# A hybrid attention / mLSTM layer on one core: the hand-over from the last head's scan to the output projection, rearranged

## The chip, the cores and the metric

The kernel runs on one core of a Trainium2 chip. The metric is the device time of one execution in microseconds (us); lower is better. Before the change the median of three runs is 1529.1 us (1527.36 to 1534.01).

A core has five engines that run side by side, each through its own list of instructions in a fixed order: PE (TensorE, matrix products into the eight PSUM banks), DVE (VectorE), ACT (ScalarE), POOL (GpSimd) and SP (SyncE, which here only issues DMA transfers). ACT and POOL issue some transfers too. An instruction whose input, or whose memory, is not yet free stops its engine and all that stands behind it in the list.

## The reference, cut to what matters

One layer works on 128 context tokens and 1024 latent tokens of width 1024, nine blocks of 128 rows; block 0 is the context. A conditioning vector gives six modulation vectors (shift, scale and gate, for each of two sub-layers), one set for context and one for latent tokens:

```python
m = jax.nn.silu(cond) @ w_ada_l + b_ada_l          # split into sh1, sc1, g1, sh2, sc2, g2
h = rmsnorm(x, norm1_w) * (1 + sc1) + sh1
...                                                # attention heads and mLSTM heads side by side, from h @ w_in
mix = jnp.concatenate([attn_o, hm], axis=-1) @ w_out
x = x + g1 * mix
h2 = rmsnorm(x, norm2_w) * (1 + sc2) + sh2
x = x + g2 * swiglu(h2, w_gu, w_down)
```

The mLSTM heads run a scan in both directions over the blocks; their result, normalised and gated, is `hm`. The first half of the rows of `w_out` belongs to attention, the second to the mLSTM heads.

## The kernel before, in words

The nine blocks are taken in three groups ("c") of three. Matrix operands are split into a high and a low part, and a product is the sum of three. The stages in order of time: modulation, first norm and the input projections; four mLSTM heads, head by head (projection, then scan), with attention for group 0 beside them; then, around 440 to 570 us of the profile, the hand-over with which the change deals; then for each group the gated feed-forward (`gate_up`, `down`), with attention and the output projection of the next group beside it.

The hand-over has these parts, which are written as Python generators and interleaved:

- The scan of the last head (`head_mlstm`). Its rows `hm` go out to memory in DRAM by POOL's queue in the end (L965).
- `attn_out_first`: the attention half of the output projection for group 0. It takes two scratch tiles in the place of two tiles of normalised input that are no longer needed: `gta` (six pieces of 128 x 512 floats: pieces 0 and 1 the gates g1 of the first 512 columns for context and latent rows, 2 and 3 those of the second, 4 the product, 5 the padded conditioning vector) and `mxa` (the split attention output of three blocks). DVE multiplies the bank by the gate into piece 4 (L1360), POOL adds that to the rows `x1a` (L1361). Later, pieces 0 and 1 serve as the landing place `spare` for weights.
- `ada_rest((5,), ...)`: the last modulation vector, g2, in two halves of 512. Each half ends with a row: a DMA on SP's queue loads the bias into the row (L477), DVE adds the product to it (L480) and halves it (L482), and ACT's queue stores it to DRAM (L483). Both halves use the same row `hmx[0:2, 512:1024]`, so the second bias load waits until the first row has been stored.
- `prefill`: the mLSTM half of the output projection for all nine blocks. For a block b, `mix(b)` turns the rows `hmr` (PE transposes, L120) and splits them into a tile `mx` (ACT L1265, DVE L141); `half(b, n)` makes the products of 512 columns (`out_block`, L1219, L1221, L1223), multiplies by the gate out of the bank into a tile `t` (`add_gated`, DVE L1180) and adds it to the rows (POOL L1181). The gate of block 0 is `gx_all`, that of the others `gl`. `end(b)` takes the squares of the rows for the second norm (`stats`, ACT L1398). `norm2` scales a block's rows (ACT L1414), turns them (PE L120), applies scale and shift (ACT L1422, DVE L1424) and splits the result (ACT L1429, and POOL for group 0, L141); before, block 0 to 2 follow `end(2)` to `end(4)`.
- `attention` for group 1 begins beside `prefill`. It loads a block's queries into a tile `qr` of which there is one (ACT's queue, L1078), turns and splits them (`qT`, L1089), and for each head makes the scores (PE L1111), their maximum (DVE L1113), the exponentials into a tile `pr` of which there are two (ACT L1114), and a split copy (ACT L1117, DVE L1118), which DMA transposes for the value products.

Two things set the order. First, a planner lays the instructions of each engine in a fixed order before the run, from its own estimate of their durations; `hot(n)` lets the instructions in its block count as n places earlier, and `issue_after` puts some behind others. Second, tiles lie in pools, and a pool's memory is used again when it has been closed. The pools of the hand-over are laid from the lower end in the order of their opening, so the tiles of `prefill` come to lie on those of `attn_out_first`; a new tile waits until the tiles under it have been read for the last time. From their sizes, in KB of each partition, counted from the start of the old input tiles:

| place | tile of `attn_out_first` | tile of `prefill`, before | `attn_out_first`, after | `prefill`, after |
|---|---|---|---|---|
| 0 to 8 | `mxa`, blocks 0 and 1 | `wq`, split weights | `gta`, pieces 0 to 3 | `wq` |
| 8 to 12 | `mxa`, block 2 | `mx`, first (`gx_all`) | `gta`, pieces 4 and 5 | `hmr`, both |
| 12 to 20 | `gta`, pieces 0 to 3 | `mx`, second and third | `mxa`, blocks 0 and 1 | `mx`, first and second |
| 20 to 24 | `gta`, pieces 4 and 5 | `hmr`, both | `mxa`, block 2 | `mx`, third |

The tiles `t` of `add_gated` come from the pool `ft` at the other end of the memory, three of them under the tag `t2`; that place was held by tiles of earlier stages.

## Time and profile before

| | us |
|---|---|
| median of three runs | 1529.1 |
| lowest and highest | 1527.36, 1534.01 |
| the profiled execution: its time | 1531.07 |
| the profiled execution: its span, first to last instruction | 1529.3 |
| PE busy in the span | 1473.0 |
| DVE, ACT, POOL busy | 1015.8, 770.4, 268.8 |
| granted clock, mean | 0.989 |

The profile is of one execution. In its rows a start is in us from the start of the span, then comes a duration, the engine, the line of the kernel, the operation, and the tiles as output<-inputs; buffer numbers are left out, so all tiles of one name share a row. What stands in brackets is the time that the engine sat idle before, and the instruction that ended the wait. "SPq" or "ACTq" is the issue of a transfer on that engine's queue; the transfer itself lands later. An `f32` product takes several passes, so one of them can count as more than one instruction. The rows by window give for each engine its busy time and, in parentheses, its instructions; then the clock that PE was granted (1.00 is full), the share of the DMA engines' time, and GB/s.

### The profile page before, as it was taken

How to read it: one execution, taken by the hardware profiler on the slowest of the kernel's cores; microseconds unless marked ns; L12 is line 12 of the kernel's file. 1: busy time of each engine (PE TensorE's matmuls, PEld its weight loads, DVE VectorE, ACT ScalarE, POOL GpSimd, SP SyncE). 2: the span in 40 equal slices, each digit the busy share in tenths (PEclk: the TensorE clock that was granted, in tenths of full speed). 3: DMA queues.
4: the chain of work that ended last, by engine and by line, in shares of the span. 5: the costliest groups of instructions: out<-in, count | busy, mean ns of one | idle time of the engine just before them, and what ended most of it. 6: DMA issues, size and time to landing. Idle time of an engine off the chain costs nothing.

```text
span 1529.3 us, 23410 instructions
## 1 busy us (share of the span) xinstructions
PE 1473.0 (96%) x8539; PEld 1244.7 (81%) x8539; DVE 1015.8 (66%) x2025; ACT 770.4 (50%) x1429; POOL 268.8 (18%) x354
## 2 busy tenths in 40 slices
PE   6899999999998899999999999999999999999997
PEld 3545567677766789999898999989998989999996
DVE  4887654838568866878637587787866585554554
ACT  4764475947654645556433444656553443323333
POOL 0113423333344441010010100100010101101110
PEclk9899999999999999999999999999999999999998
DMA  9664323523456577869635357886864445544541
GB/s 359 205 198 147 101 71 42 120 53 62 110 177 207 135 180 187 200 156 195 171 115 166 124 184 212 198 184 145 201 145 138 138 139 179 158 135 126 153 144 56
DMA packets 387113, 233.77 MB, mean 153 GB/s; under 512 B 170102, under 2 KB 347462, under 8 KB 386998
## 3 DMA queue, kind: packets, MB, share of 16 engines
q1 hardware_dynamic: 385006, 228.69, 55.0%
q10 hardware_dynamic: 1864, 3.20, 0.9%
q8 instruction: 67, 1.10, 0.3%
q14 instruction: 48, 0.39, 0.1%
q0 software_dynamic: 128, 0.39, 0.1%
HBM read 182.21 MB, written 11.69 MB: 127 GB/s over the span
## 4 chain that ended last, share of the span: by engine, by line
PE 78%; DVE 5%; DMA 3%; ACT 3%; issue 1%; POOL 1%; SPq 0%; ACTq 0%; DVEq 0%; POOLq 0%
PE mm L1437 11%; PE mm L1436 11%; PE mm L1435 11%; PE mm L1191 5%; PE mm L1192 5%; PE mm L1193 5%; PE S L1111 4%; PE wi L514 3%; PE wi L513 3%; PE wi L512 3%; PE mm L1219 2%; PE po L1136 2%; PE po L1135 2%; PE mm L1221 2%; PE mm L1223 2%
## 5 line engine op out<-in xcount | busy, mean ns | idle before, releaser
L163 ACT CAST whi<-raw 128x1024 fp32r<-128x1024 f32 x214 | 219.2, 1026 | 367.8 <-PE mm L1436 146.9
L141 DVE TENSOR_TENSOR wlo<-raw,whi 128x1024 fp32r<-128x1024 f32 x214 | 257.7, 1204 | 170.5 <-ACT whi L163 167.0
L1436 PE MATMUL mm<-aTl,whi 128*128 128x384 f32 x1056 | 354.4, 336 | 0.0
L1437 PE MATMUL mm<-aTh,wlo 128*128 128x384 f32 x1056 | 354.2, 336 | 0.0
L1435 PE MATMUL mm<-aTh,whi 128*128 128x384 f32 x1056 | 353.2, 335 | 0.0
L141 POOL TENSOR_TENSOR hl<-tn,hl 128x384 fp32r<-128x384 f32 x66 | 84.9, 1286 | 846.6 <-ACT hl L1458 796.4
L1435 PEld LDWEIGHTS mm<-aTh,whi 128*128 128x128 f32 x1056 | 198.3, 188 | 0.7
L1436 PEld LDWEIGHTS mm<-aTl,whi 128*128 128x128 f32 x1056 | 198.3, 188 | 0.6
L1437 PEld LDWEIGHTS mm<-aTh,wlo 128*128 128x128 f32 x1056 | 198.3, 188 | 0.1
L1191 PE MATMUL mm<-whi,hl 128*128 128x512 f32 x372 | 144.4, 392 | 1.1 <-DVE t L1180 1.1
L1192 PE MATMUL mm<-wlo,hl 128*128 128x512 f32 x372 | 145.1, 391 | 0.0
L1193 PE MATMUL mm<-whi,hl 128*128 128x512 f32 x372 | 142.7, 391 | 0.0
L1118 DVE SCALAR_TENSOR_TENSOR pl<-pr,st,ph 128x1152 f16<-128x1152 f32 (+1 forms) x72 | 96.9, 1346 | 37.3 <-ACT ph L1117 35.9
L1113 DVE TENSOR_REDUCE st<-S 128x1 f32<-128x1152 f32 (+1 forms) x72 | 88.9, 1234 | 17.5 <-PE S L1111 17.2
L1114 ACT ACTIVATE pr<-S,st 128x1152 f32<-128x1152 f32 (+1 forms) x72 | 81.3, 1129 | 33.0 <-DVE st L1113 28.2
L1117 ACT ACTIVATE ph<-pr,st 128x1152 f16<-128x1152 f32 (+1 forms) x72 | 83.8, 1164 | 26.3 <-issue 10.9
L1180 DVE TENSOR_TENSOR t<-mm,gl 128x512 f32<-128x512 f32 x102 | 69.1, 686 | 38.1 <-PE mm L1193 16.0
L512 PE MATMUL wi<-headw,hT 128*128 128x384 f16 x288 | 93.9, 326 | 0.2 <-ACT th L799 0.2
L513 PE MATMUL wi<-headw,hT 128*128 128x384 f16 x288 | 93.9, 326 | 0.0
L514 PE MATMUL wi<-headw,hT 128*128 128x384 f16 x288 | 93.9, 326 | 0.0
L1111 PE MATMUL S<-kst,qT 128*128 128x384 f32 (+1 forms) x400 | 84.5, 344 | 0.8 <-ACT pr L1114 0.8
L1191 PEld LDWEIGHTS mm<-whi,hl 128*128 128x128 f32 x372 | 69.9, 188 | 15.2 <-DVE t L1180 1.5
(400 smaller groups left out, 2591.3 us busy)
## 6 DMA issues: line engine op xcount, KB each, us to landing
raw<-in_w_gu_dram SPq DMA_DIRECT2D x132, 512.0 KB
raw<-in_w_down_dram SPq DMA_DIRECT2D x60, 512.0 KB
a<-in_w_ada_dram SPq DMA_DIRECT2D x24, 512.0 KB
gl<-g_d SPq DMA_DIRECT2D x36, 256.0 KB
aw<-in_w_ada_dram SPq DMA_DIRECT2D x16, 512.0 KB
iraw<-in_w_in_dram SPq DMA_DIRECT2D x32, 256.0 KB
x<-in_x_sample_dram SPq DMA_DIRECT2D x11, 512.0 KB
raw<-in_w_out_dram SPq DMA_DIRECT2D x10, 512.0 KB
```

The lines of the kernel that those rows point to most:

```text
L141: (dve if eng == "dve" else pool).tensor_tensor(out=out, in0=full, in1=hi, op=ALU.subtract)
L163: nc.scalar.copy(hi[:, :n], raw[:, :n])
L512: mm(ps[:, :n], ah, wh[:, k % 2, c0 : c0 + n], start=(k == 0), stop=False)
L513: mm(ps[:, :n], ah, wl[:, k % 2, c0 : c0 + n], start=False, stop=False)
L514: mm(ps[:, :n], al, wh[:, k % 2, c0 : c0 + n], start=False, stop=(k == KD - 1))
L1111: mm(S[:, n, 0:w], qT[:, h, :], kst[kv][:, t, c0 + n * w : c0 + (n + 1) * w], start=(t == 0), stop=(t == 1))
L1191: mm(ps, ah, wh[:, k % 2, :], start=(k == 0), stop=False)
L1192: mm(ps, ah, wl[:, k % 2, :], start=False, stop=False)
L1193: mm(ps, al, wh[:, k % 2, :], start=False, stop=(k == nk - 1))
L1435: mm(ps, wh[:, k, :], th[:, k, :], start=(k == 0), stop=False)
L1436: mm(ps, wh[:, k, :], tl[:, k, :], start=False, stop=False)
L1437: mm(ps, wl[:, k, :], th[:, k, :], start=False, stop=(k == KD - 1))
```

## The change

1. In `attn_out_first` the second bias row no longer takes the row of the first, but the first two partitions of a tile under the tag `qr`, attention's only query tile.
2. The pool of the old input tiles becomes two, opened in the order 1, 0, so `gta` and `mxa` change places; the rows `hmr` get a pool of their own, opened ahead of that of `mx`. The table above shows both.
3. The products `t` of blocks 0 and 1 in `prefill` go into two tiles under attention's tag `pr`, one for each half of the columns, block 0 in the first 512 columns of it and block 1 in the next.
4. `norm2` of blocks 0, 1 and 2 no longer follows `end(2)`, `end(3)` and `end(4)`, but `half(3, 0)`, `half(4, 0)` and `half(5, 0)`, that is half a block later in program order.

```diff
-    hTp = es1.enter_context(tc.tile_pool(name="hTp", bufs=1, reuse_waits="tile"))
+    hTp = [es1.enter_context(tc.tile_pool(name=f"hTp{c}", bufs=1, reuse_waits="tile")) for c in (1, 0)][::-1]
...
-    hT = [(hTp if c < 2 else rowp).tile([P, 2, KD, CT], F16, name=f"hT{c}", tag=f"hT{c}" if c < 2 else "b4") for c in range(NCH)]
+    hT = [(hTp[c] if c < 2 else rowp).tile([P, 2, KD, CT], F16, name=f"hT{c}", tag=f"hT{c}" if c < 2 else "b4") for c in range(NCH)]
...
-    def add_gated(x1, ps, g, n, eng=dve):
+    def add_gated(x1, ps, g, n, eng=dve, t=None):
         cs = slice(n * 512, (n + 1) * 512)
-        t = t2()
+        t = t2() if t is None else t
...
-            hm = xe.tile([P, 512], F32, name=nm("hmr"), tag="hmr", bufs=2)
+            hm = xh.tile([P, 512], F32, name=nm("hmr"), tag="hmr", bufs=2)
...
             if c < 2:
-                add_gated(x1s[c][i], ps, g, n, pool)
+                if b < 2:
+                    if b == 0:
+                        mixed["t", n] = ap2.tile([P, 3, CT], F32, name=nm("t2"), tag="pr", bufs=2).rearrange("p a n -> p (a n)")
+                    t = mixed["t", n][:, b * 512 : (b + 1) * 512]
+                else:
+                    t = None
+                add_gated(x1s[c][i], ps, g, n, pool, t)
...
-            if 2 <= b < CB + 2:
-                yield from norm2(0, cur, b - 2)
...
-        yield from end(0)
+        end(0)
...
-        yield from end(1)
+        end(1)
         for b in range(2, NB):
             load_x1(b + 2)
             half(b, 0)
             yield
+            if 3 <= b < CB + 3:
+                yield from norm2(0, cur, b - 3)
             if b + 1 < NB:
                 mix(b + 1)
                 yield
             half(b, 1)
             yield
-            yield from end(b)
+            end(b)
...
-        gt = hTp.tile([P, 6, 512], F32, name="gta", tag="hT1")
-        mx = hTp.tile([P, CB, NQ, P], F32R, name="mxa", tag="hT0")
+        gt = hTp[1].tile([P, 6, 512], F32, name="gta", tag="hT1")
+        mx = hTp[0].tile([P, CB, NQ, P], F32R, name="mxa", tag="hT0")
...
+        rows_at = [lambda: hmx[0:2, 512:1024],
+                   lambda: ap.tile([P, NQ, HD], F32, name="bias", tag="qr", bufs=1).rearrange("p h d -> p (h d)")[0:2]]
...
-                       lambda: hmx[:, 0:512], lambda: hmx[0:2, 512:1024], 1, store=nc.scalar.dma_start)
+                       lambda: hmx[:, 0:512], lambda: rows_at.pop(0)(), 1, store=nc.scalar.dma_start)
...
     homes["wq"] = ctx.enter_context(tc.tile_pool(name="wq", bufs=1, reuse_waits="tile"))
+    xh = ctx.enter_context(tc.tile_pool(name="xh", bufs=1, reuse_waits="tile"))
     xe = ctx.enter_context(tc.tile_pool(name="xe", bufs=1, reuse_waits="tile"))
```

## The prediction

> **What bounds the kernel now.** I read the page's first part, then the busy time in long stretches.
>
> ```profile
> PE 1473.0 (96%) x8539; PEld 1244.7 (81%) x8539; DVE 1015.8 (66%) x2025; ACT 770.4 (50%) x1429; POOL 268.8 (18%) x354
> ```
>
> ```profile
> 500.00:530.00 30.00, 26.36 (x116) 21.21 (x117) 25.53 (x67) 18.30 (x29) 14.81 (x10) 0.89 0.63 153
> 518.00:526.00 8.00, 7.42 (x25) 6.00 (x24) 5.15 (x20) 5.98 (x10) 3.48 (x3) 0.57 0.34 81
> 600.00:900.00 300.00, 300.00 (x1641) 275.93 (x1640) 204.31 (x296) 139.37 (x183) 24.43 (x19) 1.00 0.63 160
> ```
>
> The columns are length, then PE, PEld, DVE, ACT and POOL busy, the granted clock, DMA. From 600 to 900 PE never idles and has its full clock, so an edit there could win only by fewer matmuls, and this change removes none. A stall that goes ahead of such a stretch is kept to the end. The edits lie at 455 to 545, where the last head's scan hands over to the output projection (prefill). There PE idles 3.64 of 30 us and the clock falls to 0.57. So I read PE's timeline there; brackets give idle time and releaser.
>
> ```profile
> 482.09 1.07 PE L1223 MATMUL mm<-ir,mxa 128*128 128x512 f32 x4
> ...
> 485.37 0.66 PE L120 MATMUL mm<-ident,hmra 128*128 128x128 f32 x4
> 486.10 0.68 PE L936 MATMUL wi<-va,sd 128*128 128x129 f32 x4
> 488.60 1.19 PE L1219 MATMUL mm<-whi,mx 128*128 128x512 f32 x4 [1.81 <-ACT mx L1265]
> ...
> 490.91 1.18 PE L1223 MATMUL mm<-whi,mx 128*128 128x512 f32 x4
> 491.92 0.60 PE L120 MATMUL mm<-ident,qr 128*128 128x128 f32 x4
> ...
> 496.95 1.07 PE L1223 MATMUL mm<-whi,mx 128*128 128x512 f32 x4
> ...
> 501.12 1.20 PE L1219 MATMUL mm<-whi,mx 128*128 128x512 f32 x4 [1.61 <-DVE mx L141]
> ...
> 517.17 1.55 PE L120 MATMUL mm<-ident,y 128*128 128x128 f32 x8 [1.82 <-ACT y L1414]
> ...
> 520.15 2.04 PE L1219 MATMUL mm<-whi,mx 128*128 128x512 f32 x4 [0.57 <-DVE fl L1424]
> ...
> 567.70 0.33 PE L1435 MATMUL mm<-aTh,whi 128*128 128x384 f32 x1
> ```
>
> Four waits, 5.81 us in all: for mixing operands (1.81 and 1.61), for block 0's normalised rows (1.82), and for a bank that norm2 still holds (0.57). The half clock costs 8.00 x (1 - 0.57) = 3.4 us more. These 9.2 us are all that closing the stalls named here can give.
>
> **The change part by part.** No arithmetic instruction is added or removed; waits and places change.
>
> *First four products (t in pr).* An output block leaves its PSUM bank by DVE L1180 into a t2 tile, then POOL adds it.
>
> ```profile
> 501.93 0.67 DVE L1180 TENSOR_TENSOR t<-mm,gx_all 128x512 f32<-128x512 f32 x1
> ```
>
> ```profile
> 485.37 1.27 POOL L1361 TENSOR_TENSOR x1a<-x1a,gta 128x512 f32<-128x512 f32 x1 [0.80 <-DVE gta L1360]
> ...
> 499.03 0.58 POOL L965 DMA_DIRECT2D hm_d<-hm  x1 [0.42 <-POOL hm L960]
> 502.69 7.15 POOL L1181 TENSOR_TENSOR x1a<-x1a,t 128x512 f32<-128x512 f32 x4 [3.08 <-DVE st L1116]
> ...
> 540.29 2.55 POOL L141 TENSOR_TENSOR aTl<-fl,aTh 128x512 fp32r<-128x512 f32 x2 [1.55 <-ACT aTh L1429]
> ```
>
> ```profile
> hm_d<-hm POOLq DMA_DIRECT2D x2, 192.0 KB, 2.3
> ```
>
> The first output block left PE at 492.1 (490.91 + 1.18), yet its product ran at 501.93. The t2 memory lies at the right-hand end, where the last head's rows were: their store went out at 499.03 and lands 2.3 us later, 501.3. That reads as the wait. In a pr tile, idle since attention's block 2, the first product can run at about 492.5, the third when its block ends at 498.0 (496.95 + 1.07); the second needs gl, asked for at 492.6 (row below). So the banks come free some 4 to 9 us sooner and the wait of 1.61 at 501 goes: value 1.6, bounds 0 and 1.6. POOL's four adds, 502.69 to 509.84, start with them, and so do the statistics of block 0 (ACT, with the casts of which the next part speaks):
>
> ```profile
> 486.21 1.04 ACT L163 CAST whi<-raw 128x1024 fp32r<-128x1024 f32 x1 [1.95 <-DMA raw<-in_w_out_dram]
> ...
> 487.96 0.58 ACT L1265 CAST mx<-mm 128x512 fp32r<-128x512 f32 x1
> ...
> 500.51 1.22 ACT L1114 ACTIVATE pr<-S,st 128x1152 f32<-128x1152 f32 x1 [0.37 <-DVE st L1113]
> ...
> 508.63 1.06 ACT L1398 ACTIVATE jk<-x1a 128x1024 bf16<-128x1024 f32 x1 [4.61 <-POOL x1a L1181]
> ...
> 516.41 1.32 ACT L1414 ACTIVATE y<-x1a,ry 128x512 f32<-128x512 f32 x2
> ```
>
> The square waited 4.61 us for POOL; its result reached y at 516.41, 7.8 us after it began. If the square starts at about 501.5, y comes near 509.3, and PE at 515 doesn't wait for it: 1.82 + 0.57 = 2.4, bounds 0 and 2.4.
>
> What this adds: the first two heads' exponentials (ACT, L1114) wait for the pr tiles until the POOL adds of those t are done; behind them in ACT's queue stand casts and squares, for which DVE and PE wait. The first head's tile needs two adds of about 1.8 (7.15 for four), begun near 493 and 498, so done near 500; its exponential starts at 500.51 now. Covered: 0, bounds 0 and a loss of the second gap's 1.6.
>
> *norm2 half a block later.* Its instructions stay 800 places ahead in priority, so the planner puts them where their inputs are ready, as before; I take 0. Bounds: a gain of 1.8 (already in the term above) and no loss, because gate_up, the reader, begins at 567.70, 25 us after the last norm2 subtraction ends at 542.84 (540.29 + 2.55).
>
> *Places exchanged.* Mixing tile 0 lay on the gates' tile gta, last read by POOL until 486.64 (485.37 + 1.27). After, it lies on mxa, last read by PE until 483.16 (482.09 + 1.07). So block 0's ACT cast can run when its transposes end, 486.03, instead of 487.96, if the planner puts it ahead of the weight cast at 486.21, which sat on ACT waiting for its DMA. Ahead: PE starts by 486.7 and the whole 1.81 goes. Behind: nothing. I take half, 0.9. The weight cast would run 0.58 later, for output blocks that come after 492: 0. The weight slot wq, after the change on the gates, is free at 486.64; the second of the two weight casts of this pair, which uses it, can't start before the first's end at 487.25: 0. The hmr tiles stay on the same parts of gta, so their issue at 486.67 stays.
>
> *Second bias row in the query tile.*
>
> ```profile
> 466.10 1.02 SPq L1369 DMA_DIRECT2D hmra<-hm_d  x2
> 468.77 0.27 SPq L477 DMA_DIRECT2D hmx<-in_b_ada_dram  x1
> 469.09 0.39 SPq L162 DMA_DIRECT2D gta<-in_w_out_dram  x1
> 486.67 0.34 SPq L1236 DMA_DIRECT2D hmr<-hm_d  x1
> 492.60 0.84 SPq L1211 DMA_DIRECT2D gl<-g_d  x2
> ```
>
> ```profile
> 468.33 0.69 DVE L1360 TENSOR_TENSOR gta<-mm,gta 128x512 f32<-128x512 f32 x1 [0.44 <-PE mm L1223]
> ```
>
> SP stands from 467.12 to 468.77 (1.65) for the first row's store. Behind it is the load into gta, which must wait anyway for the last reader of those gates, until 469.02: it was issued at 469.09. So 0; the upper bound is 1.6. On the other side, the query tile was loaded far ahead:
>
> ```profile
> 345.74 0.33 ACTq L1078 DMA_DIRECT2D qr<-q_d  x1
> ```
>
> ```profile
> 489.15 0.25 ACTq L483 DMA_DIRECT2D g_d<-hmx  x1
> ```
>
> ```profile
> 476.52 3.71 DMA gta<-in_w_out_dram
> ```
>
> If the bias row takes the slot first, the load has to follow the row's store: 489.15 + 2.3 (the nearest store) + 3.7 (the nearest load, twice as large) = 495.2, and attention's transposes, at 491.92 today, come 3.3 us later. PE then has the output blocks up to 498 to do, if they are ahead in its queue; ACT, which issues the load, would stand up to 2.3 with casts behind it. I take 0; bounds 0 and a loss of 3.3 plus another half clock.
>
> *The sum.* 1.6 + 2.4 + 3.4 = 7.4 is what PE could save in 500 to 530. But DVE is busy 25.53 of those 30 us, a share of 0.85. Three products of 0.67 move ahead of 500, leaving 23.5, which doesn't fit into 22.6. I take a share halfway between 0.85 and 1, 0.925: 23.5 / 0.925 = 25.4 us. So I count 30 - 25.4 = 4.6 and the 0.9: 5.5. Against the profiled execution's 1531.07 (span 1529.3 and 1.8 around it) that is 1525.6. That execution lies 2.0 above the median of the runs, 1529.1, so I carry the difference over: **1523.6**.
>
> *A rule of the clock.* The granted clock fell to 0.51 in 518 to 520, after this:
>
> ```profile
> 486.00:488.00 2.00, 0.71 (x5) 0.52 (x4) 1.93 (x5) 1.79 (x5) 0.64 (x1) 1.00 0.97 387
> 488.00:490.00 2.00, 1.40 (x6) 1.18 (x7) 2.00 (x5) 1.75 (x5) 0.00 (x0) 1.00 0.85 261
> 514.00:516.00 2.00, 1.35 (x8) 0.99 (x6) 1.73 (x15) 1.79 (x2) 0.00 (x0) 1.00 0.00 0
> 516.00:518.00 2.00, 0.83 (x6) 0.63 (x7) 2.00 (x5) 1.87 (x5) 0.33 (x1) 1.00 0.99 120
> 518.00:520.00 2.00, 1.57 (x8) 1.17 (x6) 2.00 (x7) 1.17 (x3) 0.94 (x1) 0.51 0.87 180
> ```
>
> PE was busy 2.11 of 4 us at 486 to 490 and kept its clock, 2.18 of 4 at 514 to 518 and lost it. So a gap of that size costs the clock once in two here, and closing it is a chance, not a certainty. The Trainium skill, TensorE: Matmul & The Clock Gate, "HAM oscillation", puts the rule at no idle gaps over about 3.4 us. By it the 1.82 us gap would not be the cause, and closing it would leave the half clock: at most 1.6 + 2.4 + 0.9 = 4.9 saved, 1524.2, and the second rival would weigh more. The trace disagrees with the plain rule, as no gap here is that long; the page's free-running window would fit the two unlike outcomes.
>
> **The rivals.** (1) *All closes*: attention's share of DVE's work slips behind 530, where PE has other work, and PE saves 0.9 + 0.9 + 7.4 = 9.2: 1519.9. For it: in 600 to 900 DVE is busy 204 of 300, so there is room to catch up. Against: block 0's chain to y runs through DVE too. (2) *The clock still drops*, because another wait (for a mixing operand or attention's first scores) takes its place: only about 1.5 stays, 1527.6. For it: ACT and DVE are nearly full there. (3) *Slower, through the query tile*: PE meets attention's transposes in its queue before their rows have landed. Price 3.3 and a half clock of 3.4 with no gap closed: 1535.8. It decides if the planner leaves them ahead of output blocks 2 and 3, at 491.9, and the rows land later than 492; each us past that costs one. (4) *The planner's order shifts further on*: its estimated timeline moves, and a later hand-over (there are two more) gets a wait and a clock drop like those of 515, 5.8 each; both give +11.6 - 5.5 = +6.1, 1535.2; with the third rival's 3.3, 1538.5. Against: PE is full for hundreds of us around them. (5) *The change does not do what it says*, because the waits have other causes: 1529.
>
> **How the numbers follow.** The forecast and its neighbours (1521.5 to 1526) 0.42; all closes 0.14; clock still drops or no effect 0.20; query tile 0.13; shifted order 0.11. 0.5% is 7.6 us, about what a measurement of this kernel can tell from no change: below 1521.5 only the first rival, 0.14; above 1536.7 the tails of the third and fourth, 0.16 with what I can't see in the planner's order; between, 0.70. The range 1519 to 1537 leaves out about 0.05 below and 0.15 above. The forecast's own range is 1521 to 1526.
>
> **What would show it.** Right: the first L1180 near 492 to 494 and the fourth before 503; POOL's first adds before 500; y of block 0 before 511; no half clock between 510 and 530; the bias row issued near 467; the first L1219 on mx at 486.7 (place exchange worked) or 488.6 (it didn't); gate_up's first matmul about 5 us before 567.7 and the same span behind it. Wrong: PE waiting for qr at 492 or ACT standing behind its load; first products still at 502 (then another tile held them); a half clock elsewhere in 480 to 567; or new PE idle time after 600.

## The result, and the profile after

The kernel after takes 1534.8 us (median of 12 runs, 1532.4 to 1538.13); the kernel before, run beside it on the same chip, takes 1530.84 us (12 runs, 1527.36 to 1534.23). The ratio is **1.003, 95% interval [1.0019, 1.0041]**. That is 4.0 us slower, where 5.5 us less were forecast. The time lies in the range that was given, 1519 to 1537, but the change has the other sign. The profiled execution of after took 1534.57 us, its span is 3.5 us longer than that of before:

```profile
span 1532.8 us, 23405 instructions
...
PE 1473.3 (96%) x8539; PEld 1244.0 (81%) x8539; DVE 1023.2 (67%) x2025; ACT 769.9 (50%) x1429; POOL 270.8 (18%) x354
```

PE has the same work (1473.3 against 1473.0 us), so all but 0.3 of the 3.5 us is idle time. DVE, with the same 2025 instructions, is busy 7.4 us longer. That becomes a clue below.

The start of the hand-over itself moves by up to 4.6 us from one profile to the next (481.96 to 486.57 in the 20 kernels' profiles). The clock ahead of it is a large part of that: counted as length x (1 - granted clock), its drops up to the mark cost 8.5 us in after and 13.7 in after_later, whose mark is the latest, with the same idle time of 36 us. So stages have to be compared from a mark of their own. I use three marks on PE: the end of the last product on `mxa` (483.16 before), the first `gate_up` product (567.70) and the first `down` product (606.23); a fourth, the first transposes of the next norm2, at 874.38. The columns are those of the rows by window in the prediction. First before, then after:

```profile
483.16:567.70 84.54, 78.53 (x400) 63.24 (x400) 66.59 (x149) 45.08 (x74) 38.57 (x29) 0.96 0.66 169
567.70:606.23 38.53, 38.09 (x228) 37.40 (x227) 22.01 (x29) 18.98 (x25) 5.54 (x5) 1.00 0.69 194
```

```profile
482.41:569.62 87.21, 79.29 (x400) 64.03 (x400) 72.65 (x149) 44.74 (x74) 40.06 (x29) 0.96 0.63 160
569.62:610.17 40.55, 38.23 (x227) 37.47 (x226) 22.78 (x29) 18.88 (x25) 6.13 (x5) 1.00 0.74 200
```

Read the first two numbers of each row, length and PE busy. The hand-over is 2.67 us longer, the stage behind it 2.02 us longer, and the long stage behind that, to the fourth mark, is the same (268.15 and 268.16 us, PE busy throughout). With the mark itself 0.75 us earlier and the rest of the span 0.45 shorter (1529.3 - 874.38 = 654.92 against 1532.8 - 878.33 = 654.47) the sum is 3.5. PE's idle time (length less busy) went from 6.01 to 7.92 us in the hand-over and from 0.44 to 2.32 us behind it: 3.8 together. So in this pair of profiles no idle time came far away; half of it is where the edits are, half in the 40 us that follow. A stage's length holds the clock as well, and that falls otherwise in other profiles of the same order, as the experiments show; the idle time is the steadier number.

PE's timeline of after, the rows that answer to those of before and the waits that are new:

```profile
481.79 0.62 PE L1223 MATMUL mm<-ir,mxa 128*128 128x512 f32 x2
...
487.50 2.01 PE L1219 MATMUL mm<-whi,mx 128*128 128x512 f32 x4 [1.50 <-ACT mx L1265]
...
493.03 1.19 PE L1219 MATMUL mm<-whi,mx 128*128 128x512 f32 x4 [0.47 <-DVE mx L141]
...
496.07 0.66 PE L120 MATMUL mm<-ident,qr 128*128 128x128 f32 x4
...
514.78 1.33 PE L1111 MATMUL S<-kst,qT 128*128 128x384 f32 x6 [1.39 <-ACT pr L1114]
...
516.68 0.66 PE L120 MATMUL mm<-ident,y 128*128 128x128 f32 x4 [0.57 <-ACT y L1422]
...
532.89 1.20 PE L1219 MATMUL mm<-whi,mx 128*128 128x512 f32 x4 [1.12 <-ACT mx L1265]
...
537.92 0.63 PE L120 MATMUL mm<-ident,y 128*128 128x128 f32 x4 [1.71 <-DVE mx L141]
...
581.71 0.27 PE L1135 MATMUL po<-phT,vs 128*128 128x256 f16 x1 [2.01 <-DMA phT<-ph]
```

The wait of 1.61 us at 501 is gone, and the 1.82 us for `y` shrank to 0.57. In their place stand 1.39 us for the bank of the scores, 1.12 and 1.71 us near 535, and, in the stage behind, 2.01 us for the transposed probabilities of block 3's last pair of heads. The last one was there before too, with 0.44 us:

```profile
579.94 0.28 PE L1135 MATMUL po<-phT,vs 128*128 128x256 f16 x1 [0.44 <-DMA phT<-ph]
```

**Why `y` did not come early.** The products did what was forecast; DVE's and POOL's timelines of after show what else happened:

```profile
492.96 0.68 DVE L1180 TENSOR_TENSOR t<-mm,gx_all 128x512 f32<-128x512 f32 x1
...
495.63 0.17 DVE L131 TENSOR_SCALAR rv<-ssh 128x3 f32<-128x3 f32 x1 [0.47 <-ACT jkh L952]
...
496.47 0.68 DVE L1180 TENSOR_TENSOR t<-mm,gx_all 128x512 f32<-128x512 f32 x1
...
497.25 1.29 DVE L137 SCALAR_TENSOR_TENSOR ry<-rt,ry 128x3 f32<-128x3 f32 x1
...
501.00 0.16 DVE L137 SCALAR_TENSOR_TENSOR ry<-rt,ry 128x3 f32<-128x3 f32 x1
...
504.26 0.68 DVE L1180 TENSOR_TENSOR t<-mm,gl 128x512 f32<-128x512 f32 x1
...
505.78 0.16 DVE L1115 RECIPROCAL st<-st 128x1 f32<-128x1 f32 x1 [0.84 <-ACT pr L1114]
505.98 0.15 DVE L1116 TENSOR_SCALAR st<-st 128x1 f32<-128x1 f32 x1
...
514.21 1.34 DVE L135 TENSOR_TENSOR rt<-ry 128x1 f32<-128x1 f32 x2
```

```profile
497.23 1.30 POOL L1181 TENSOR_TENSOR x1a<-x1a,t 128x512 f32<-128x512 f32 x1 [1.10 <-DVE rt L136]
501.30 0.83 POOL L960 TENSOR_TENSOR hm<-hm,ry 128x384 f32<-128x384 f32 x1 [2.78 <-DVE ry L137]
502.09 1.30 POOL L1181 TENSOR_TENSOR x1a<-x1a,t 128x512 f32<-128x512 f32 x1
503.33 0.58 POOL L965 DMA_DIRECT2D hm_d<-hm  x1
505.03 1.29 POOL L1181 TENSOR_TENSOR x1a<-x1a,t 128x512 f32<-128x512 f32 x1 [1.12 <-DVE t L1180]
...
514.19 1.27 POOL L1181 TENSOR_TENSOR x1a<-x1a,t 128x512 f32<-128x512 f32 x1 [3.55 <-DVE ry L137]
```

The small DVE instructions from 495.63 to 501.16 (501.00 + 0.16) are the reciprocal square root of the last head's tail. An early product (496.47) and the casts of attention's queries, which now come here, stand between them, and one step of 0.16 us took 1.29, from 497.25 to 498.54, because POOL's early add ran from 497.23 to 498.53. POOL then does the tail's multiplication at 501.30, one more early add, and sends the last head's rows at 503.33; before it sent them at 499.03. So the edit that frees `t` from the wait for this store makes the store itself 4.3 us late. ACT's timeline of after, here and for block 3:

```profile
504.44 1.22 ACT L1114 ACTIVATE pr<-S,st 128x1152 f32<-128x1152 f32 x1 [3.27 <-DVE st L1113]
505.65 1.05 ACT L1406 ACTIVATE jk<-x1a 128x1024 bf16<-128x1024 f32 x1
...
515.91 1.33 ACT L1422 ACTIVATE y<-x1a,ry 128x512 f32<-128x512 f32 x2 [1.18 <-DVE ry L137]
...
570.95 1.23 ACT L1114 ACTIVATE pr<-S,st 128x1152 f32<-128x1152 f32 x1 [4.65 <-DVE st L1113]
...
575.55 1.05 ACT L163 CAST whi<-raw 128x1024 fp32r<-128x1024 f32 x1 [3.29 <-DMA raw<-in_w_gu_dram]
576.50 1.25 ACT L1117 ACTIVATE ph<-pr,st 128x1152 f16<-128x1152 f32 x1
```

Block 0's square `jk` stands on ACT right behind attention's first exponential, and that came at 504.44 instead of 500.51, since the transposes of the queries came 4.2 us later (496.07, before 491.92). So the square began at 505.65, 3 us sooner than before and not the 7 that were counted on, and from there to `y` it took 10.3 us instead of 7.8. Of the gain 0.5 us is left.

**Why there is a longer wait at 581.71.** The last three of ACT's rows above are the chain that feeds it: the exponential of the last head, a weight cast for `gate_up`, and the cast `ph`, whose transposing load PE waits for. ACT works in order. The weight cast waits 3.29 us for its transfer, and `ph` stands behind it, 5.55 us after its exponential began. Before, `ph` came first, 1.78 us after it:

```profile
571.05 1.23 ACT L1114 ACTIVATE pr<-S,st 128x1152 f32<-128x1152 f32 x1
...
572.83 1.26 ACT L1117 ACTIVATE ph<-pr,st 128x1152 f16<-128x1152 f32 x1 [0.47 <-ACT pr L1114]
575.08 1.05 ACT L163 CAST whi<-raw 128x1024 fp32r<-128x1024 f32 x1 [0.99 <-DMA raw<-in_w_gu_dram]
```

Yet this lateness is not what made the first wait longer. Here is SP's issue of the transposing load, before and after:

```profile
574.11 2.71 SPq L1120 DMA_TRANSPOSE phT<-ph  x1
```

```profile
577.78 1.68 SPq L1120 DMA_TRANSPOSE phT<-ph  x1
```

Count from the first `gate_up` product. `ph` began 6.88 us after it instead of 5.13, and the load was issued at 8.16 instead of 6.41, both 1.75 late. But from its issue to the product that waited for it the load took 3.93 us instead of 5.83, so that product ran at 12.09 instead of 12.24: the operand came no later than before. What moved is the place of the value products in PE's own list. 57 `gate_up` products instead of 67 stand ahead of them, at 0.17 us each, so PE was ready for them at 10.08 us instead of 11.80, and the wait grew from 0.44 to 2.01. No edit touches these instructions. The planner orders by its own timeline, and with the edits that timeline puts the weight cast ahead of `ph` and fewer products ahead of the value products.

### The profile page after: what moved, and what is told of

It is laid out like the page before. It is cut to its first block, busy times and chain, and to the rows that moved or that the text cites. A ratio compares the mean times of both kernels' runs of the same rounds, so it can differ in the third digit from the quotient of the medians.

```text
span 1532.8 us, 23405 instructions
## 1 busy us (share of the span) xinstructions
PE 1473.3 (96%) x8539; PEld 1244.0 (81%) x8539; DVE 1023.2 (67%) x2025; ACT 769.9 (50%) x1429; POOL 270.8 (18%) x354
## 4 chain that ended last, share of the span: by engine, by line
PE 78%; DVE 7%; ACT 3%; DMA 3%; issue 1%; POOL 0%; SPq 0%; ACTq 0%; DVEq 0%; POOLq 0%
PE mm L1445 11%; PE mm L1444 11%; PE mm L1443 11%; PE mm L1191 5%; PE mm L1192 5%; PE mm L1193 5%; PE S L1111 4%; PE wi L514 3%; PE wi L513 3%; PE wi L512 3%; PE po L1136 2%; PE mm L1219 1%; PE po L1135 1%; PE mm L1221 1%; PE mm L1223 1%; DMA plT<-pl 1%
```

## The experiments

Eighteen kernels were run, each timed against the kernel before on the same chip. "Hand-over" and "stage after" are the windows between the marks above, of each profiled execution; "cast between" says whether a weight cast stands between the exponential and `ph` of block 3's last head, "ahead" how many `gate_up` products stand ahead of the value products that read its `phT`; idle is PE's, length less busy; the clock is the mean granted one. The stage after had a clock of 1.00 in all kernels but after_ph (0.96).

| kernel | cast between | ahead | ratio [95%] | hand-over: length, idle, clock | stage after: length, idle |
|---|---|---|---|---|---|
| before | no | 67 | 1 | 84.5, 6.0, 0.96 | 38.53, 0.4 |
| only_place | no | 67 | 0.9996 [0.9983, 1.0010] | 84.9, 6.6, 0.96 | 38.90, 0.8 |
| place_bias | no | 67 | 0.9999 [0.9986, 1.0012] | 86.4, 7.6, 0.96 | 38.68, 0.6 |
| t_bias | no | 67 | 1.0003 [0.9990, 1.0016] | 85.6, 7.3, 0.96 | 38.34, 0.3 |
| **after** | yes | 57 | 1.0030 [1.0019, 1.0041] | 87.2, 7.9, 0.96 | 40.55, 2.3 |
| no_bias | yes | 57 | 1.0021 [1.0009, 1.0033] | 85.0, 8.1, 0.98 | 40.99, 2.8 |
| no_norm2 | yes | 59 | 1.0032 [1.0020, 1.0044] | 85.9, 6.9, 0.96 | 40.25, 2.2 |
| no_t | yes | 57 | 1.0033 [1.0020, 1.0047] | 84.8, 9.0, 1.00 | 41.17, 2.9 |
| no_place | yes | 57 | 1.0032 [1.0021, 1.0043] | 86.2, 9.3, 0.98 | 40.01, 1.8 |
| bias_alone | yes | 59 | 1.0032 [1.0016, 1.0048] | 87.8, 8.9, 0.96 | 40.82, 2.8 |
| t_alone | yes | 59 | 1.0020 [1.0008, 1.0032] | 85.7, 7.2, 0.96 | 40.59, 2.5 |
| after_jk | yes | 57 | 1.0025 [1.0012, 1.0039] | 85.9, 8.3, 0.98 | 40.56, 2.3 |
| after_tailfirst | yes | 57 | 1.0032 [1.0017, 1.0046] | 87.0, 8.8, 0.96 | 41.31, 3.1 |
| after_ph | no (moved) | 57 | 1.0019 [1.0004, 1.0033] | 87.6, 8.5, 0.96 | 42.87, 3.0 |
| after_late | yes | 83 | 1.0010 [0.9998, 1.0023] | 86.0, 8.4, 0.98 | 40.21, 1.9 |
| after_later | yes | 100 | 1.0015 [1.0002, 1.0028] | 84.5, 8.5, 1.00 | 38.75, 0.3 |
| t_late | yes | 83 | 1.0005 [0.9993, 1.0016] | 85.5, 7.1, 0.96 | 40.05, 1.8 |
| t_later | yes | 100 | 1.0020 [1.0008, 1.0032] | 85.2, 8.0, 0.98 | 39.06, 0.5 |
| before_late | no | 83 | 0.9992 [0.9978, 1.0007] | 85.9, 5.8, 0.94 | 38.16, 0.0 |
| before_later | no | 100 | 0.9997 [0.9987, 1.0007] | 86.2, 6.2, 0.94 | 38.21, 0.0 |

### One part taken back at a time

If one part carries the loss, the kernel without it is as fast as before. Each diff is against after, cut to the lines that matter.

*no_bias*, the second bias row back in its old place:

```diff
-                       lambda: hmx[:, 0:512], lambda: rows_at.pop(0)(), 1, store=nc.scalar.dma_start)
+                       lambda: hmx[:, 0:512], lambda: hmx[0:2, 512:1024], 1, store=nc.scalar.dma_start)
```

> The changed kernel with the second bias row back in the place of the first; the other three parts stay. Theory Q (the query tile: attention starts late because the row holds its only query tile until about 491, and the lost 3.5 us come from there): attention's transposes of the queries come before 493 again, its first exponential before 502 instead of 504.4, and the time is 1531 or less. Theory N (norm2 moved half a block is what costs): no change, 1534 to 1536. Theory O (none of the parts as such: the planner writes another order each time, and a few us more or less come with it): the query transposes come early and the time still is not 1531, or it is and the same happens when any other part is left out.

*no_norm2*, norm2 back behind the block's end:

```diff
+            if 2 <= b < CB + 2:
+                yield from norm2(0, cur, b - 2)
...
-            if 3 <= b < CB + 3:
-                yield from norm2(0, cur, b - 3)
```

> The changed kernel with norm2 back where it was; the other three parts stay. Theory Q: attention's queries still come at about 496, the time stays at 1534 to 1536. Theory N: the waits at 533 to 538 of PE for y and for a mixing operand behind norm2 go, and the time is 1531 or less. Theory O: anything between 1528 and 1537, without either sign.

*no_t*, the products back in `t2` tiles:

```diff
-                add_gated(x1s[c][i], ps, g, n, pool, t)
+                add_gated(x1s[c][i], ps, g, n, pool)
```

> The changed kernel with the first four products back in t2 tiles; the other three parts stay. If the products in the pr tiles bring what the prediction counted on (products near 493 instead of 502), taking them away costs 2 us or more: 1537 and above, and the first product is at about 502 again. Theory Q and N: they don't own the loss, so 1535 or above. Theory D (the pr tiles held by the products delay the first two heads' exponentials): 1532 or less.

*no_place*, the tiles back in their old places:

```diff
-        gt = hTp[1].tile([P, 6, 512], F32, name="gta", tag="hT1")
-        mx = hTp[0].tile([P, CB, NQ, P], F32R, name="mxa", tag="hT0")
+        gt = hTp.tile([P, 6, 512], F32, name="gta", tag="hT1")
+        mx = hTp.tile([P, CB, NQ, P], F32R, name="mxa", tag="hT0")
```

> The changed kernel with the places of the gates' tile and of the mixing operands as before and the rows hmr in the old pool; the other three parts stay. If the exchange gives nothing (block 0's cast still stands behind the weight cast, PE's first mixing block at 487.5 against 488.6), the time stays at 1534 to 1536; if it gave the 1.1 us by which that block starts sooner, 1536. Theory O: a move of 2 us or more either way.

Measured: 1.0021, 1.0032, 1.0033, 1.0032, all four intervals above 1. No part carries the loss by itself: whichever is taken back, it stays. That speaks against the third rival of the prediction (the query tile) as much as against `t`: in no_bias the transposes of the queries come at 492.50 again, but the first exponential only at 505.62 (before 502 was expected), and the time stays. In no_t the first product is back at 501.80, and taking the early products away costs nothing, where 2 us were expected if they brought what the prediction counted on. What the four share with after, and before has not, is the long wait near 580 (2.38, 2.15, 2.83 and 1.45 us), and with it two marks of the order: on ACT the weight cast between the exponential and `ph`, on PE 57 or 59 products ahead instead of 67.

### Three attempts to mend a link of the chain

*after_ph* puts the fourth weight cast behind block 3's last `ph`:

```diff
-                    act(phv, prv, AF.Copy, scale=st[:, 3:4])
+                    loaded["ph"] = act(phv, prv, AF.Copy, scale=st[:, 3:4]).ins
...
-                for _ in range(4):
-                    next(main)
+                for q in range(4):
+                    with behind("ph") if c == 0 and q == 3 else nullcontext():
+                        next(main)
```

> The changed kernel, with one edge more: on ACT the fourth weight cast of the first gate_up stands behind the split copy of attention's last head of block 3. In the changed kernel the cast stood ahead of it and held it for 3.3 us while its weights came, and PE then waited 2.0 us at 581 for that head's transposed copy. Theory W (this flip of two instructions in the planner's order, which all four kernels with one part left out have too and the kernel before does not, is worth 1.6 of the lost 3.5 us): the split copy follows its exponentials by 2 us as before, PE's wait there falls below 0.6, and the span is 1.6 shorter: about 1533 in time. Theory Q (query tile) and O (no single cause): the wait moves to another place and the time stays at 1534 to 1536.

`ph` came 3.3 us sooner, at 573.2, yet SP issued the transposing load only at 576.04, behind others in its queue, and PE had its operand only 7 us later. PE's timeline of after_ph:

```profile
582.99 0.27 PE L1135 MATMUL po<-phT,vs 128*128 128x256 f16 x1 [3.04 <-DMA phT<-ph]
```

A wait below 0.6 us was expected; it grew to 3.04, and behind it the clock fell (0.96 on the mean of this stage, 1.00 in all the other kernels). So the cast's place does not make this wait by itself: here no cast stands between, but still 57 products ahead, and PE stood longer than in after. Whether the wait is the loss this run does not tell.

*after_jk* takes block 0's square off the memory of the last head's rows:

```diff
-            jk = ft.tile([P, D], BF16, name=nm("jk"), tag="t2", bufs=3)
+            jk = ft.tile([P, D], BF16, name=nm("jk"), tag="t2", bufs=3) if at is None else ap2.tile([P, D], BF16, name=nm("jk"), tag=at, bufs=2)
```

> The changed kernel, with the scratch output of block 0's sum of squares in a free pl tile instead of a t2 tile; nothing else, and every engine keeps its order. Theory S (the squares of block 0 waited for the memory of t2, not for their input: that memory is held until the last head's rows have been stored, and the store went out at 503.3 instead of 499.0): the square starts earlier than 505.65 by the time that ACT stands for it, 0 to 1.2 us, as the exponentials of the first head stand ahead of it until 505.7; if theory S is the whole of it the y of block 0 comes before 515 and 0.5 to 1 us is won. Rival (DVE's queue, full at 0.99 from 510 to 530, sets when y comes): y at 515.5 to 516, no gain.

1.0025, and `y` no sooner. The order on ACT stayed, and there the square still began with the end of the first exponential: what held it was not the memory.

*after_tailfirst* puts the four early products behind the last head's tail on DVE:

```diff
+                    loaded["tail"] = loaded["rsqrt"]
...
-                add_gated(x1s[c][i], ps, g, n, pool, t)
+                with behind("tail") if b < 2 else nullcontext(), behind("store") if b < 2 else nullcontext():
+                    add_gated(x1s[c][i], ps, g, n, pool, t)
```

> The changed kernel, with the first four products and their sums behind the last head's closing work on DVE and POOL (its reciprocal roots and its store). Theory T (the early products were put into DVE's and POOL's queues ahead of that work, and so the store went out 4.3 us later, and with it all that waits for the memory under it: the loads of the next rows at 505.6 instead of 501.3, the squares): the store goes out at 499 to 500, the loads of rows at 501 to 502, and PE reaches gate_up 1 to 2 us sooner than 569.6. Rival: the store comes early again, and PE reaches gate_up at 569 to 570 anyhow, because nothing behind the store sets PE's time.

1.0032. Counted from the end of the last product on `mxa`, the store went out at 17.3 us instead of 20.9 (15.9 before), but the first `gate_up` product came at 86.98 instead of 87.21, where 1 to 2 us sooner was expected. The tail's lateness does occur, but taking it away gave nothing back. The planner's order changed with this edit in other places too, so it is not a test of the tail alone.

### The parts alone and in pairs

The diffs are against before, cut in the same way. *only_place* is the change of places, *bias_alone* the bias row, *t_alone* the products; *place_bias* and *t_bias* are two of them together.

```diff
-        gt = hTp.tile([P, 6, 512], F32, name="gta", tag="hT1")
-        mx = hTp.tile([P, CB, NQ, P], F32R, name="mxa", tag="hT0")
+        gt = hTp[1].tile([P, 6, 512], F32, name="gta", tag="hT1")
+        mx = hTp[0].tile([P, CB, NQ, P], F32R, name="mxa", tag="hT0")
```

> The kernel before with the exchange of places alone. Theory W: here the planner leaves the split copy of the last head of block 3 ahead of the weight cast, so PE's wait near 580 stays below 0.6 and nothing is lost: 1529 to 1532 where the kernel before has 1531. What the exchange can give is 0.9 to 1.8 us at block 0's mixing operand, if its cast moves ahead of the weight cast. Theory O: any change of the order costs 3 us or so: 1534.

```diff
-                       lambda: hmx[:, 0:512], lambda: hmx[0:2, 512:1024], 1, store=nc.scalar.dma_start)
+                       lambda: hmx[:, 0:512], lambda: rows_at.pop(0)(), 1, store=nc.scalar.dma_start)
```

> Only the second bias row in the spare query tile; in the order of this kernel a gate_up weight cast stands ahead of the last head's probability cast on ScalarE, as in the kernel after. Theory W (the place of that cast costs the stage from the first gate_up product to the first down product about 2 us, 38.5 us before against 40.6 after): the stage takes 40 to 41 us and the ratio to before is 1.001 to 1.003. Theory Q (the later query load costs by itself, in the hand-over): from the last modulation product to the first gate_up product 86 us or more against 84.5, the stage after it 38.5 to 39. Theory N (neither, the loss needs all four parts): 84.5 and 38.5, ratio 1.000.

> The same with the places exchanged as well; here the planner puts no gate_up weight cast ahead of the last head's probability cast. Theory W: the stage from the first gate_up product to the first down product takes 38.5 to 39 us, and the ratio is 1.000, whatever the query tile does. Theory Q: the hand-over takes 86 us or more, as with the bias row alone, ratio 1.001 to 1.002. Theory N: 84.5 and 38.5, ratio 1.000.

```diff
-                add_gated(x1s[c][i], ps, g, n, pool)
+                add_gated(x1s[c][i], ps, g, n, pool, t)
```

> Only the first blocks' gated products in the tiles of the probabilities, with the output blocks ahead of the normalisation as before; the cast stands ahead. Theory W: the stage after the first gate_up product takes 40 to 41 us, ratio 1.001 to 1.003. Theory T (the early products delay the last head's store by 4 us, 503.33 after against 499.03 before, and that costs the hand-over): from the last modulation product to the first gate_up product 86 us or more, the stage after it 38.5 to 39. Theory N: 84.5 and 38.5, ratio 1.000.

> The gated products in the tiles of the probabilities and the second bias row in the query tile; no cast stands ahead. Theory W: the stage after the first gate_up product takes 38.5 to 39 us; what is left is the hand-over's, and with 84.5 there the ratio is 1.000. Theories Q and T: the hand-over takes 86 to 87.2 us as in the kernel after, ratio 1.001 to 1.002, with the stage after it at 38.5 to 39. Theory N: 84.5 and 38.5.

The pairs turn the question round: the bias row alone costs 0.32%, and with a second edit on top nothing; the products alone cost 0.20%, and with the bias row on top, which alone costs more, nothing. Costs that belonged to the edits would add, unless one edit undid the cost of another. What goes with the loss is the order: with 57 or 59 products ahead the stage after takes 40.01 us or more, with 67 it takes 38.90 or less, and the ratios go with it. The cast between goes the same way, except in after_ph. In all these kernels PE had the operand 11.5 to 13.2 us after the first `gate_up` product, with the cast between or without it; it was ready at 10.1 with 57 ahead, at 10.4 with 59, at 11.8 with 67. So theory W named the right kernels, by the wrong one of the two marks. The rows of t_bias by window, then its ACT and PE timelines:

```profile
482.88:568.45 85.57, 78.25 (x400) 63.32 (x400) 71.99 (x149) 45.46 (x74) 38.19 (x29) 0.96 0.66 171
568.45:606.79 38.34, 38.09 (x227) 37.39 (x226) 22.00 (x29) 18.99 (x25) 5.50 (x5) 1.00 0.69 193
```

```profile
501.16 1.07 ACT L1406 ACTIVATE jk<-x1a 128x1024 bf16<-128x1024 f32 x1
...
510.68 1.34 ACT L1422 ACTIVATE y<-x1a,ry 128x512 f32<-128x512 f32 x2 [0.89 <-DVE ry L137]
...
571.97 1.23 ACT L1114 ACTIVATE pr<-S,st 128x1152 f32<-128x1152 f32 x1
...
573.75 1.26 ACT L1117 ACTIVATE ph<-pr,st 128x1152 f16<-128x1152 f32 x1 [0.47 <-ACT pr L1114]
```

```profile
516.94 1.84 PE L1111 MATMUL S<-kst,qT 128*128 128x384 f32 x6 [1.98 <-ACT pr L1114]
```

`ph` again begins 1.78 us after its exponential. And this kernel does what the prediction wanted of `t`: its planner put the square ahead of the exponential, it began at 501.16 (501.5 was said) and `y` at 510.68 (509.3 was said). PE no longer waits for block 0's `y`. Yet the ratio is 1.0003, and PE is idle 7.3 us in this hand-over instead of 6.0: another wait, 1.98 us for the bank of the scores, took the place of the 1.82. DVE is busy 71.99 us there, nearly as long as after (72.65) and 5.4 longer than before.

Theories Q and T, which put the loss into the query load and the late store, fall with the pairs; theory N falls with the parts alone. Q's sign in the hand-over did appear, 87.82 us in bias_alone and 86.44 in place_bias, but the latter's ratio is 0.9999 (its profiled execution, 1535.22 us, lies 3.6 above its median). T's did not: 85.69 us in t_alone, 85.58 in t_bias, where 86 or more was said.

### Taking the wait away

Here one number changes, the priority of the last value products of block 3, so that more `gate_up` products stand ahead of them on PE; up to there the order is the same. *after_late* and *after_later* are against after, *t_late* and *t_later* against t_alone, *before_late* and *before_later* against before. The number is 170 in the first of each two (83 products ahead) and 145 in the second (100):

```diff
-                        with hot(hv):
+                        with hot(170 if b == 3 and j == 3 else hv):
```

> The kernel after with one priority changed: the last value products of block 3 stand behind 83 gate_up products on TensorE instead of 57; the gate_up weight cast still stands ahead of the last head's probability cast on ScalarE. Theory W (the 2.01 us wait for the transposed probabilities at 581.71 is the loss of the stage after the first gate_up product): no wait there, 38.2 to 38.7 us from the first gate_up product to the first down product against 40.55 after and 38.53 before, and the ratio falls from 1.003 to 1.0015 or below. Theory C (the stage is longer for another reason, the weights' casts or loads, and the wait only shows it): a wait for weights takes its place, the stage stays at 40 us or more, ratio 1.003.

> The same priority in the kernel that has only the gated products in the tiles of the probabilities (40.59 us in that stage, a wait of 2.51 us, ratio 1.0020). Theory W: no wait, 38.2 to 38.7 us, ratio 1.0005 or below, that is as before. Theory C: 40 us or more, ratio 1.002.

> The same priority in the kernel before, where the wait was 0.44 us (83 products ahead instead of 67). Theory W: 38.1 us in that stage instead of 38.53, ratio 0.9995 to 1.000. Theory C: 38.5 us, ratio 1.000. A ratio of 0.998 or less would say that the priority itself brings something which has nothing to do with the wait, and the two other runs would then be read against it.

The wait did not go, it went over to the second transposed tile, as PE's timeline of after_late shows:

```profile
587.34 0.27 PE L1136 MATMUL po<-plT,vs 128*128 128x256 f16 x1 [1.91 <-DMA plT<-pl]
```

So the stage kept 40.21 us, which was forecast wrongly; yet the ratio fell to 1.0010. In t_late it was the same, 1.75 us and 1.0005. In before_late no wait is left (38.16 us), though PE comes there just as early. At this second tile the lateness of the chain does show: its load was issued 11.86 us after the first `gate_up` product in after_late and 9.47 in before_late. Hence the second three:

> The kernel after with the last value products of block 3 behind 100 gate_up products instead of 57 (83 in the run before this one, where the wait of 1.91 us went over from the first to the second transposed tile). At 0.167 us for a product they are reached 17.3 us after the first gate_up product, and the second transposed tile landed at 16.8 us. Theory W: no wait of over 0.3 us in the stage, 38.1 to 38.5 us from the first gate_up product to the first down product, ratio below that of the run before it, 1.0010. Theory C: a wait for weights or an eviction takes its place, 40 us or more, ratio 1.001 or above.

> The same in the kernel with the gated products alone (40.59 us and 1.0020 as it was; 40.05 us with a wait of 1.75 us and 1.0005 at 83 products). Theory W: no wait, 38.1 to 38.5 us, ratio 1.000 or below. Theory C: 40 us or more, ratio 1.0005 or above.

> The same in the kernel before, which had no wait left at 83 products (38.16 us, ratio 0.9992): 38.1 to 38.2 us, ratio 0.9990 to 1.0000 by either theory. More than 38.5 us would say that the later place itself costs something.

Now the wait is gone; 0.33 us in after_later and 0.52 in t_later, for rows of the next queries, are what PE still stands. The rows by window of after_later:

```profile
486.57:571.10 84.53, 76.04 (x401) 61.55 (x401) 72.58 (x147) 44.75 (x74) 39.98 (x29) 1.00 0.66 165
571.10:609.85 38.75, 38.42 (x227) 36.31 (x226) 21.62 (x28) 18.78 (x25) 6.46 (x5) 1.00 0.72 203
```

The stage is 1.8 us shorter than after's 40.55, and 1.5 in t_later (39.06 against 40.59): the 2 us of this stage are the wait for the transposed probabilities. The control lost nothing by the later place (38.21 us, 0.9997). The rest of the forecast failed: 38.1 to 38.5 us were said, and ratios below 1.0010 and at most 1.000; they are 1.0015 and 1.0020. So the whole loss is not gone. The four kernels with late value products have ratios of 1.0005 to 1.0020, 1.0013 on the mean, where after and t_alone have 1.0030 and 1.0020, 1.0025 on the mean. About half the loss goes with the wait, but by intervals of ±0.0012 each the share is not settled, and t_alone and t_later, both at 1.0020, show no fall at all (the profiled execution of t_later, 1531.58 us, was the shortest of its runs, so its profile says little on its median).

**What stays open** is where the rest of the loss lies. PE's idle time points to the hand-over: in after it is 1.9 us longer there than before, and in the kernels with a cast between it is 6.9 to 9.3 us, in those without it 5.8 to 7.6 (after_ph aside). But the length of the hand-over does not tell the two kinds apart, 84.5 to 87.8 us against 84.5 to 86.4. Up to the first `gate_up` product after, after_late and after_later have one order and 7.9 to 8.5 us of idle time, yet they took 87.2, 86.0 and 84.5 us, at a clock of 0.96, 0.98 and 1.00; before, before_late and before_later took 84.5, 85.9 and 86.2 at 0.96, 0.94 and 0.94. So the 2.67 us between the two profiles at the top are in part the luck of the clock, and that the rest of the loss is the hand-over's idle time is likely, not shown: it is made of other waits in each kernel, and no run takes one of these away by itself. Why the orders that bring fewer products ahead also leave more idle time 30 to 80 us earlier was not found. No kernel beat the one before: the lowest ratio, 0.9992 for before_late, has 1 within its interval.

## Why the prediction was wrong, by its steps

Two steps failed: the term for block 0's `y` with the clock, which brought nothing, and the stage behind the hand-over, put at "the same span", which cost 2 us. They explain why nothing was gained and about half of the loss; where the other half comes from stays open.

**First four products: right in what they do, wrong in what that gives.** The first product ran at 492.96 (492.5 said), POOL's adds start before 500, the fourth product ran at 504.26 (before 503 said), and the gap of 1.61 is gone; of it 0.47 came back at 493.03. **The step that failed is the term of 2.4 us for `y`**, with the clock's 3.4 that was hung on it: "if the square starts at about 501.5, y comes near 509.3". The square started at 505.65, behind an exponential that came 3.9 us later than before; and the 7.8 us from there to `y` were taken over from before as if DVE's queue stayed as it was, and became 10.3. `y` came at 515.91, PE's transposes 0.5 us sooner than before. And t_bias, where `y` did come at 510.68, shows that the value of the term was wrong as well as its condition: the wait passed to the scores' bank, and the time did not fall.

**DVE's load as a limit: the sum held its work constant.** 25.5 us less the products that move was to fit into 25.4. The same 149 instructions of the hand-over took 72.65 us instead of 66.59. With the old places of the products it is 66.6 to 67.9 in seven kernels, with the new one 69.0 to 72.8 in all the others. For the exponentials the prediction weighed only their wait for the `pr` tiles; the scores' wait of 1.39 us at 514.78 is for an exponential that had waited 3.49 us for DVE. The 7.4 us that the limit was set against were also 0.3 too many: the gap of 1.61 began at 499.51, so PE's 3.64 us of idle time and the clock's 3.4 are all there was from 500 to 530.

**The clock term: not saved, only moved.** The half clock of 518 to 526 is gone, and two others came; they are counted below and cost 3.4 us, as the one before did. This is the second rival's condition. In other profiles of the same order they cost 0 to 3.4 us, so a sum of waits could not have settled this term.

**Places exchanged: 0.9 said, nothing that can be told came.** From the mark to the first product on `mx` it was 5.44 us (488.60 - 483.16) and is 5.09 (487.50 - 482.41), but in other kernels with the exchange it is up to 5.78 (after_late). The cast still stands behind the weight cast, the "behind" case of the prediction. Alone the edit gives 0.9996.

**Second bias row: right that PE does not wait for the rows.** Attention's transposes came at 496.07 (495.2 said) and stood behind another output block; PE did not stand for them (in no_t and no_place it did, for 0.90 and 0.61 us). But the 0 was meant for the time, and alone this edit costs 0.32% [0.16, 0.48] by the order that it brings about.

**norm2 later: 0 is not refuted.** Without it the ratio is 1.0032 against 1.0030.

**The stage behind: "the same span" was wrong.** The fourth rival had the mechanism, the planner's order shifting further on, but at a later hand-over with a wait and a half clock of 5.8 each. It came 10 us after the hand-over, as 2 us: PE reached value products that no edit touches 1.72 us sooner, behind 57 products instead of 67, and their operand came no sooner. That the rival's 1535.2 is near the measured time is a coincidence of its price.

## What to carry to other kernels

When a planner orders the instructions, price an edit with the order that comes out, not with the trace of the order before: here the number of products that the order puts ahead of one waiting product went with the time in every combination of the edits that was run, and the edits themselves did not. When a wait grows, count from one common mark when the operand came and when the engine was ready for it; here a cast that was clearly late in the chain suggested itself as the cause, and it was the engine that had come sooner. When work is moved earlier on a full engine, ask whose chain it now interrupts. And compare stages by idle time and clock apart: one profile's length mixes them.

## What the runs showed of the hardware

**DVE and POOL hold each other up.** In the rows above, DVE's step at 497.25 took 1.29 instead of 0.16 us and ended with POOL's add (498.54 and 498.53); at 514.21 two such steps took 1.34 beside an add from 514.19 to 515.46. A reciprocal and a scalar product at 505.78 and 505.98 ran beside an add from 505.03 to 506.32 in 0.16 and 0.15. The ones held up read two operands from SBUF, the others one. POOL loses too: its add at 508.43 took 2.21 us instead of 1.29, with a DVE subtraction of two SBUF operands running from 508.26 to 509.48. The Trainium skill, "SBUF — State Buffer", "Who interferes with whom", says that a DVE instruction with two SBUF inputs contends with a GpSimd instruction that reads SBUF, and that the port pair they share is an exclusive lock. The trace agrees, and this is where most of DVE's 6 us went: in the hand-over of after, seven such steps of 0.16 us took 1.1 to 1.3, 7.5 us more among them, where before it was three steps and 2.6 us. Adds were moved into the middle of chains of small two-input steps.

**The clock fell after shorter gaps than before.** The rows by window of after, the granted clock in the column behind POOL:

```profile
484.00:486.00 2.00, 1.96 (x10) 0.94 (x8) 1.97 (x5) 0.88 (x1) 1.28 (x1) 1.00 1.04 401
486.00:488.00 2.00, 0.49 (x1) 0.44 (x2) 1.97 (x5) 2.00 (x6) 0.00 (x0) 0.90 0.95 322
488.00:490.00 2.00, 2.00 (x6) 1.57 (x5) 2.00 (x5) 0.80 (x3) 0.57 (x1) 0.50 0.71 202
490.00:492.00 2.00, 2.00 (x10) 1.52 (x10) 1.00 (x2) 0.34 (x1) 0.99 (x1) 0.75 0.80 228
...
538.00:540.00 2.00, 2.00 (x9) 1.68 (x10) 0.37 (x1) 0.00 (x0) 1.28 (x1) 0.70 0.77 148
540.00:542.00 2.00, 2.00 (x8) 1.91 (x8) 0.78 (x2) 0.00 (x0) 1.17 (x1) 0.50 0.00 0
542.00:544.00 2.00, 2.00 (x12) 1.71 (x11) 1.88 (x2) 1.23 (x2) 0.11 (x1) 0.95 0.02 7
```

It fell within 486 to 488, around a gap of 1.50 us, with PE busy 2.45 of the last 4 us; in the same place before, a gap of 1.81 us with 2.11 of 4 left it at 1.00. Counted as 2.00 x (1 - clock), the two drops cost 1.7 us each. Neither the length of the gap nor the busy share of 4 us tells the cases apart, so here a closed gap is not a closed drop; and after_later, with the same order and a gap of 1.53 us at the same place, had no drop in the hand-over at all (clock 1.00). The plain rule of the Trainium skill that the prediction weighed ("TensorE: Matmul & The Clock Gate", "HAM oscillation": no idle gaps over about 3.4 us) again does not tell the drops in this trace, for no gap of the hand-over was that long.

**A transposing load's landing varied by 3 us.** From SP's issue to the product that waited for it there were 3.93 us in after (577.78 to 581.71), 5.83 before (574.11 to 579.94) and 6.95 in after_ph (576.04 to 582.99). What made the difference is open.
